# A hybrid decoder block on one core: seven products for one more unit, and two small moves from VectorE and the transfers to ScalarE and GpSimd

## The chip, the cores and the metric

The kernel runs on one core of a Trainium2 chip as one launch. The metric is the device time in microseconds (us); with one core it is that core's time. Each number is a median of runs; beside it stands one profiled execution of the same kernel, whose own time is given with its span. Engines are named as the profile does: PE is TensorE's matmul stream and PEld its weight loads, DVE is VectorE, ACT is ScalarE, POOL is GpSimd, SP is SyncE. An engine name with a q (SPq, POOLq) is the sequencer or queue that issues transfers. Five of them matter here: PE, DVE, ACT, POOL and SP's queue of loads and stores.

## The reference, cut to what matters

A sequence of 528 rows (16 meta tokens and 512 inputs, 1024 wide) is normalised and projected by one matrix `w_in` into ten parts. The first eight units of work are the eight heads of differential attention, the other eight are pairs of heads of stick-breaking attention. Both branches are gated, projected, merged and normalised.

```python
proj = jnp.einsum('bld,dn->bln', h, w_in[i])
q_d, k_d, v_d, g_d, q_s, k_s, v_s, g_s, m_d, m_s = jnp.split(proj, IN_OFFSETS, axis=-1)
...
lam = jnp.exp(jnp.sum(lp[0] * lp[1])) - jnp.exp(jnp.sum(lp[2] * lp[3])) + lam_init
...
s = jnp.einsum('bhcqd,bhckd->bhcqk', q, k).astype(jnp.float32) * (DIFF_HEAD_DIM ** -0.5)
alibi = -slopes[:, None, None] * dist.astype(jnp.float32)[None]
s = jnp.where(dist >= 0, s + alibi[None, :, None], -jnp.inf)
p = jax.nn.softmax(s, axis=-1)
a = p[:, :, 0] - lam * p[:, :, 1]
return jnp.einsum('bhqk,bhkd->bhqd', a.astype(v.dtype), v)
```

A differential head has two queries and two keys of 64 columns (c = 0 and 1), two softmax maps, and one map that is used: the first minus `lam` times the second.

## The kernel before, in words

The normalised input lies transposed in SBUF as a rounded half and a remainder (`hTh`, `hTl`), so that a product of full precision is made of three products of the rounded kind: high by high, high by low, low by high. Weights come as half tiles of 128 x 4 x 128 into tiles `raw` and are split in the same way: ACT casts the high half (L185), DVE subtracts it for the low half (L190). `prep` does this four half tiles ahead of their use and `fetch` issues the next loads on SP's queue as ring buffers come free. `names` and `items` list the half tiles in the order of use; a `rawk` tile is loaded and then has another half tile added to it, by an adding transfer on POOL's queue (L147, through `added` and `placed`).

The sixteen units follow one another. While unit u computes its scores and values, the projections of the units ahead run between its small matmuls: keys and values of unit u+1, the query of unit u+2 (`stage_q`), now and then a gate. For the units below `SEVEN`, keys and values are two plain projections (`stage_k`, `stage_v`), each of two halves of 264 columns and 24 matmuls a half (L515), 96 matmuls for a unit. From the unit `SEVEN` on, `stage_kv` makes keys and values together in seven block products of twelve matmuls (L700), 84 for a unit, in Strassen's manner: the weights' half tiles and the input's quarters are added beforehand, and the results combined by DVE (L717, L720, L722). Its input sums are made once: `input_sums(k)` for k = 0 to 3 (a POOL copy, four DVE operations of 264 columns in place in `hF`, an ACT cast into `tS`, a DVE remainder into `tl`). `SUMS_AT` says in which unit and at what point each runs, `SEVEN` also when the ring of `rawk` tiles opens (three units ahead).

`stage_q` ends with both parts of a query scaled by 0.125: ACT writes the rounded one into `A[0]`, DVE the remainder into `low` (L621, L622). The head needs them in other partitions; three transfers of 64x512 on SP's queue carry them: the second head's rounded part to `A[1][LO]`, and the two remainders to `A[1][HI]` and `A[0][HI]` (L624).

`d_scores` does the four blocks of 128 query rows, longest first (528, 400, 272, 144 keys). For each block and map: scores on PE (L764), DVE adds the bias and takes the minimum (L844), ACT takes the exponential with its row sum (L848). After both maps: the reciprocal of both sums (L852), the second map by its reciprocal and by -lambda (`nlam`, L853), and the sum of the first by its reciprocal with that (L854) into `apad`. The transposes (L776) turn `apad` for the product with the values. POOL computes the bias of the next head (L829).

Each engine's list is fixed when the program is built: a scheduler places the instructions by their dependences and its own estimate of time, `run` interleaves the steps at the points given by numbers (`TD`, `SUMS_AT`), and `keep_order` ties the instructions of PE, DVE, ACT, POOL and SP in that sequence. On the chip each engine goes through its list in order; what is not ready holds what stands behind it. The core's three banks `pj` in PSUM rotate among the projections.

Of the kernel before, what the change touches and what calls it, by code (L numbers as in the profile page):

```python
# [12 lines left out]
AF = mybir.ActivationFunctionType  # L13
ALU = mybir.AluOpType
# [14 lines left out]
AOFF = [0, 416, 832, 1248]  # L29
# [6 lines left out]

ORDERED = [mybir.EngineType.PE, mybir.EngineType.DVE, mybir.EngineType.Activation, mybir.EngineType.Pool]
WARM = 12
SEVEN = 4
SUMS_AT = {0: [8.0], 1: [5.0, 11.0], 2: [8.0]}  # L40
TD = [(0.85, 11.0, 14.5), (0.95, 13.0, 16.5)]
GATE_AT = {4: 0, 5: 1, 6: 2, 7: 3, 8: 4, 11: 5, 14: 6}
LO, HI = slice(0, 64), slice(64, 128)
# [3 lines left out]
def hybrid_block_kernel(ctx: ExitStack, tc: tile.TileContext, x, meta, emb_g, emb_b, w_in, b_gate,  # L47
                        diff_lambda, subln_g, w_br_d, w_br_s, w_out, ln_g, ln_b, out):
    nc = tc.nc
    v, s, g, pe = nc.vector, nc.scalar, nc.gpsimd, nc.tensor  # L50
# [22 lines left out]
    for u, (kind, n) in enumerate(UNITS):  # L73
        if u + 1 < len(UNITS):
            other, i = UNITS[u + 1]
# [15 lines left out]
    for n, (kind, i) in enumerate(seq):  # L91
        if kind in ("BD", "BS", "wd", "ws"):
# [6 lines left out]
            o = len(loads)  # L99
# [124 lines left out]
    def placed(work, engines=ORDERED):  # L224

        ins = nc.cur_bb.bb.instructions
        n = len(ins)
        work()
        for e in engines:
            new = next((i for i in ins[n:] if i.engine == e), None)  # L230
            old = next((ins[m] for m in range(n - 1, max(n - 400, 0), -1) if ins[m].engine == e), None)
            if new is not None and old is not None:
                follow(new, old)
# [54 lines left out]
    nlam = const.tile([P, 1], F32, name="nlam")  # L288
# [297 lines left out]
    with tc.tile_pool(name="att", bufs=1) as ap:  # L586
# [22 lines left out]
        def stage_q(unit, kind, n):  # L609

            res = []
            yield from proj_tok(res, "q" + kind, n)
            ps = res[0]
            A = [apool.tile([P, S], F32R, tag=f"A{c}", name=f"A{c}") for c in range(2)]
            if diag:
                if len(diag) == 1:
                    diag.append(ap.tile([P, L], F32R, tag="bias", name="low", bufs=2))
                low = diag[1][:, :S]
            else:
                low = gpool.tile([P, S], F32R, tag="sg", name="low")  # L620
            s.activation(A[0], ps, AF.Copy, scale=0.125)  # L621
            v.scalar_tensor_tensor(low, ps, 0.125, A[0].bitcast(F32), op0=ALU.mult, op1=ALU.subtract)  # L622
            for o, src in ((A[1][LO], A[0][HI]), (A[1][HI], low[HI]), (A[0][HI], low[LO])):
                nc.sync.dma_start(o.bitcast(F32), src.bitcast(F32))  # L624
            unit["A"] = A
            yield 0.64
# [192 lines left out]
        def d_scores(unit, h):  # L819

            A = unit["A"]


            bias = ap.tile([P, L], F32, tag="bias", name="bias", bufs=2)
            if h == 0:
                g.iota(bias, pattern=[[-1, L]], base=400, channel_multiplier=1, allow_small_or_imprecise_dtypes=True)
                g.affine_select(bias, bias, pattern=[[-1, L]], compare_op=ALU.is_ge, fill=1e30, base=400,
                                channel_multiplier=1)
            g.tensor_scalar(bias, biases[-1] if h else bias, 0.5 if h else -0.5, None, op0=ALU.mult)  # L829
            biases.append(bias)  # L830
            a = apads[h % 2]
            mn = ap.tile([P, NB, 2, 2], F32, tag="mn", name="mn", bufs=2)
            zs = ap.tile([P, NB, 2], F32, tag="zs", name="zs", bufs=2)
            rz = ap.tile([P, NB, 2], F32, tag="rz", name="rz", bufs=2)
            for i in reversed(range(NB)):
                nk = NKEY[i]
                e = [E[c][:, ZOFF[i]:ZOFF[i] + nk] for c in range(2)]
                for c in range(2):
                    m = mn[:, i, c, :]
                    for n, (ps, k0, use) in enumerate(logits(A[c], K[c], i)):  # L840
                        if n == 1:
                            yield
                        b0 = 384 - P * i + k0
                        v.tensor_tensor_reduce(e[c][:, k0:k0 + use], ps[:, :use], bias[:, b0:b0 + use], -1.0, 3e38,  # L844
                                               ALU.add, ALU.min, m[:, n:n + 1])
                    if nk > 512:
                        v.tensor_tensor(m[:, 0:1], m[:, 0:1], m[:, 1:2], op=ALU.min)
                    s.activation(e[c], e[c], AF.Exp, scale=-1.0, bias=m[:, 0:1], accum_out=zs[:, i, c:c + 1])  # L848
                    if c == 0:
                        yield  # L850
                r = rz[:, i, :]
                v.reciprocal(r, zs[:, i, :])  # L852
                v.tensor_scalar(e[1], e[1], r[:, 1:2], nlam, op0=ALU.mult, op1=ALU.mult)  # L853
                v.scalar_tensor_tensor(a[:, AOFF[i]:AOFF[i] + nk], e[0], r[:, 0:1], e[1], op0=ALU.mult, op1=ALU.add)  # L854
                yield

        def d_values(unit, ta):
# [114 lines left out]
        for u, (kind, n) in enumerate(UNITS):  # L972
# [11 lines left out]
            if u in SUMS_AT:  # L984
                if not tS:
                    tS.append(ypool.tile([P, KT, L], F32R, tag="ys", name="tS"))
                steps += [(t, lambda k=u + (u > 1) + m: placed(lambda: input_sums(k))) for m, t in enumerate(SUMS_AT[u])]
            if u in GATE_AT and u < 14:
                proj.append(raw_gate(GATE_AT[u], kept["r"][GATE_AT[u]]))
            if kind == "d":  # L990
# [167 lines left out]
    for p in range(4):  # L1158
        steps = []
# [118 lines left out]
```

## Time and profile before

| what | value |
| --- | --- |
| median of three runs | 706.77 us (705.07 to 707.03) |
| profiled execution, own time | 705.09 us |
| its span | 703.3 us |
| PE busy | 693.3 us, 99% of the span |
| DVE busy | 569.5 us, 81% |
| ACT busy | 440.5 us, 63% |
| POOL busy | 129.8 us, 18% |
| data moved by DMA | 124.93 MB, mean 178 GB/s |

Shares are of the span. "Busy" counts the time in which at least one instruction of that engine runs. Groups of instructions are read as: line, engine, operation, output <- inputs, shape, count | busy us, mean ns of one | idle time of the engine just before them and who ended it. A row of waits is: engine, tile, line <- releaser: us in all, times, longest. A row of the timeline is: start us, us, the rest. A row of busy time in a stretch has its length and then PE, PEld, DVE, ACT, POOL (each with its count), the granted clock, the DMA share and GB/s.

### The profile page before, as it was taken

The page shows a single profiled execution, that of the slowest core. Times are in us where ns is not written, and L with a number is a line of the kernel's source. Part 1 is how long each engine was busy: PE and PEld are TensorE (multiplying, and loading weights), DVE is VectorE, ACT ScalarE, POOL GpSimd, SP SyncE. Part 2 cuts the span into 40 slices and gives each one's busy share as a digit, 9 for nine tenths or more (in the row PEclk, how much of TensorE's full clock was granted, in tenths as well). Part 3 has the DMA queues.
Part 4 walks back from the last instruction along what each step waited for, and adds up shares of the span by engine and source line. Part 5 has one row for each costly group of instructions (what it writes and reads, how often), then busy time and mean ns, then how long its engine had stood idle before and what let it go on. Part 6 is the DMA issues. An engine that isn't in the chain of part 4 may idle for free.

```text
span 703.3 us, 13282 instructions
## 1 busy us (share of the span) xinstructions
PE 693.3 (99%) x4478; PEld 634.1 (90%) x4478; DVE 569.5 (81%) x1225; ACT 440.5 (63%) x1073; POOL 129.8 (18%) x140
## 2 busy tenths in 40 slices
PE   8999999999999999999999999999999999999996
PEld 8999999989899898999989899988888998999885
DVE  6887998878786777899887898977666888688887
ACT  6676767767566687777757687766555456555400
POOL 2243112222222201212121220000012201230011
PEclk9999999999999999999999999999999999999999
DMA  9399557988888796899898977547477749697702
GB/s 292 103 195 182 145 117 178 212 177 184 221 186 182 188 195 183 173 223 206 207 192 219 203 152 194 164 124 242 137 165 142 148 121 245 136 174 194 264 25 116
DMA packets 184215, 124.93 MB, mean 178 GB/s; under 512 B 8994, under 2 KB 168131, under 8 KB 184147
## 3 DMA queue, kind: packets, MB, share of 16 engines
q1 hardware_dynamic: 148050, 102.84, 50.5%
q0 software_dynamic: 35776, 20.19, 23.0%
q10 hardware_dynamic: 320, 1.06, 0.4%
q8 instruction: 35, 0.57, 0.3%
q14 instruction: 34, 0.27, 0.1%
HBM read 93.54 MB, written 9.44 MB: 146 GB/s over the span
## 4 chain that ended last, share of the span: by engine, by line
PE 93%; ACT 2%; SPq 1%; DVE 1%; DMA 1%; issue 0%; DVEq 0%; ACTq 0%
PE q L700 18%; PE ps L501 12%; PE ps L499 12%; PE ps L500 12%; PE q L1083 11%; PE pso L1206 6%; PE ps L515 6%; PE sc L764 6%; PE t L776 4%; PE tv L733 1%; PE av L931 1%; PE av L932 1%; DMA raw<-in_w_in_dram 1%; PE av L925 1%; PE av L933 1%; DMA xt<-in_x_dram 1%
## 5 line engine op out<-in xcount | busy, mean ns | idle before, releaser
L190 DVE TENSOR_TENSOR w<-raw,w 128x512 fp32r<-128x512 f32 x168 | 114.3, 689 | 37.7 <-ACT w L185 36.4
L500 PE MATMUL ps<-hTl,w 128*128 128x512 f32 x368 | 144.9, 394 | 0.0
L499 PE MATMUL ps<-hTh,w 128*128 128x512 f32 x368 | 144.7, 393 | 0.0
L501 PE MATMUL ps<-hTh,w 128*128 128x512 f32 x368 | 144.7, 393 | 0.0
L185 ACT CAST w<-raw 128x512 fp32r<-128x512 f32 x168 | 103.5, 627 | 11.6 <-PE ps L501 5.4
L147 POOL DMA_DIRECT2D rawk<-in_w_in_dram x48 | 66.1, 1630 | 119.5 <-DMA rawk<-in_w_in_dram 66.1
L700 PE MATMUL q<-tS,w 128*128 128x264 f32 x384 | 82.6, 289 | 0.0
L1083 PE MATMUL q<-gh,w 128*128 128x256 f32 x448 | 81.4, 283 | 0.2 <-ACT t L1092 0.2
L501 PEld LDWEIGHTS ps<-hTh,w 128*128 128x128 f32 x368 | 69.2, 188 | 13.5
L500 PEld LDWEIGHTS ps<-hTl,w 128*128 128x128 f32 x368 | 69.2, 188 | 13.1
L499 PEld LDWEIGHTS ps<-hTh,w 128*128 128x128 f32 x368 | 69.2, 188 | 13.0
L1083 PEld LDWEIGHTS q<-gh,w 128*128 128x128 f32 x448 | 70.2, 192 | 0.5 <-ACT t L1092 0.4
L764 PE MATMUL sc<-k,A 128*128 128x264 f32 (+3 forms) x320 | 66.0, 299 | 0.0
L700 PEld LDWEIGHTS q<-tS,w 128*128 128x128 f32 x384 | 63.7, 189 | 0.3
L1083 PE MATMUL q<-gl,w 128*128 128x256 f32 x224 | 63.5, 283 | 0.0
L700 PE MATMUL q<-hTh,w 128*128 128x264 f32 x288 | 60.8, 286 | 0.0
L916 DVE TENSOR_TENSOR_SCAN e<-e,diag 128x528 f32<-128x528 f32 (+1 forms) x64 | 54.2, 850 | 5.6 <-ACT e L910 5.6
L700 PE MATMUL q<-tl,w 128*128 128x264 f32 x192 | 54.9, 286 | 0.0
L764 PEld LDWEIGHTS sc<-k,A 128*128 128x128 f32 x320 | 50.1, 189 | 2.2
L515 PE MATMUL ps<-hTh,w 128*128 128x264 f32 x256 | 51.5, 289 | 0.2 <-ACT k L642 0.2
L700 PEld LDWEIGHTS q<-hTh,w 128*128 128x128 f32 x288 | 47.8, 189 | 1.0
L781 ACT CAST ah<-t 128x384 fp32r<-128x384 f32 (+2 forms) x72 | 34.3, 477 | 21.7 <-PE t L776 21.6
(284 smaller groups left out, 1572.1 us busy)
## 6 DMA issues: line engine op xcount, KB each, us to landing
raw<-in_w_in_dram SPq DMA_DIRECT2D x142, 256.0 KB, 3.4
rawk<-in_w_in_dram POOLq DMA_DIRECT2D x48, 256.0 KB, 5.7
rawk<-in_w_in_dram SPq DMA_DIRECT2D x36, 256.0 KB, 4.1
k<-ks SPq DMA_DIRECT2D x60, 132.0 KB, 3.0
raw<-in_w_out_dram SPq DMA_DIRECT2D x16, 256.0 KB, 4.0
k<-ks SPq DMA_DIRECT2D x60, 66.0 KB, 2.7
A<-low SPq DMA_DIRECT2D x28, 128.0 KB, 3.1
raw<-in_w_br_diff_dram SPq DMA_DIRECT2D x12, 256.0 KB, 3.3
```

The lines of the kernel that those rows point to most:

```text
L147: second[l] = [lambda raw=raw, x=x: g.dma_start(raw, x, accum_op=ALU.add) for x in more]
L185: s.copy(wh, raw)
L190: eng.tensor_tensor(wl, raw, wh.bitcast(F32), op=ALU.subtract)
L499: pe.matmul(ps, wh[:, k % 4, :], hTh[:, k, M:], start=(k == 0), stop=False)
L500: pe.matmul(ps, wh[:, k % 4, :], hTl[:, k, M:], start=False, stop=False)
L501: pe.matmul(ps, wl[:, k % 4, :], hTh[:, k, M:], start=False, stop=(k == KT - 1))
L515: pe.matmul(ps[:, :H2], a[:, k % 4, :], b[:, k, ts(c, H2)], start=(k == 0 and m == 0), stop=(k == KT - 1 and m == 2))
L700: pe.matmul(bank, a[:, k, :], b, start=start and k == 0 and j == 0, stop=k == 3 and j == 2, skip_group_check=not start)
L764: pe.matmul(ps[:, :n], q, K[:, m, k0:k0 + n], start=(m == 0), stop=(m == 1))
L916: v.tensor_tensor_scan(rev, rev, diag[0][:, L - nk:][:, ::-1], 0.0, ALU.mult, ALU.max)
L1083: pe.matmul(bank, a[:, k, :], b[:, n, k, :], start=start and k == 0 and m == 0, stop=k == 3 and m == 2, skip_group_check=not start)
L1206: pe.matmul(ps, MH[k][:, ts(t, P)] if m == "h" else ML[:, k, ts(t, P)], WO[c]["hl".index(w)][:, k, r], start=(n == 0), stop=(n == 3 * KT - 1))
```

## The change

Four edits. `SEVEN` goes from 4 to 3, so that the fourth unit (differential head 3) gets its keys and values from seven products. `SUMS_AT` now places two input sums in unit 0 and two in unit 1 (before one, two and one in units 0, 1 and 2), and the index of a sum is counted accordingly. In `stage_q` ACT writes the second head's rounded query part from PSUM into `A[1][LO]`, in place of the transfer from `A[0][HI]`. In `d_scores` POOL multiplies the second map's reciprocal by -lambda, ACT multiplies the first map by its reciprocal in place, and DVE's last operation takes the second map by that product plus the scaled first map; the separate DVE multiply of the second map is gone. Lines behind these edits move down by one or two in the changed kernel (L854 there is POOL's multiply, L855 ACT's scaling, L856 the addition).

```diff
-SEVEN = 4
-SUMS_AT = {0: [8.0], 1: [5.0, 11.0], 2: [8.0]}
+SEVEN = 3
+SUMS_AT = {0: [7.0, 12.0], 1: [4.0, 9.0]}
...
             s.activation(A[0], ps, AF.Copy, scale=0.125)
+            s.activation(A[1][LO], ps[HI], AF.Copy, scale=0.125)
             v.scalar_tensor_tensor(low, ps, 0.125, A[0].bitcast(F32), op0=ALU.mult, op1=ALU.subtract)
-            for o, src in ((A[1][LO], A[0][HI]), (A[1][HI], low[HI]), (A[0][HI], low[LO])):
+            for o, src in ((A[1][HI], low[HI]), (A[0][HI], low[LO])):
                 nc.sync.dma_start(o.bitcast(F32), src.bitcast(F32))
...
                 r = rz[:, i, :]
                 v.reciprocal(r, zs[:, i, :])
-                v.tensor_scalar(e[1], e[1], r[:, 1:2], nlam, op0=ALU.mult, op1=ALU.mult)
-                v.scalar_tensor_tensor(a[:, AOFF[i]:AOFF[i] + nk], e[0], r[:, 0:1], e[1], op0=ALU.mult, op1=ALU.add)
+                g.tensor_tensor(r[:, 1:2], r[:, 1:2], nlam, op=ALU.mult)
+                s.activation(e[0], e[0], AF.Copy, scale=r[:, 0:1])
+                v.scalar_tensor_tensor(a[:, AOFF[i]:AOFF[i] + nk], e[1], r[:, 1:2], e[0], op0=ALU.mult, op1=ALU.add)
...
-                steps += [(t, lambda k=u + (u > 1) + m: placed(lambda: input_sums(k))) for m, t in enumerate(SUMS_AT[u])]
+                steps += [(t, lambda k=2 * u + m: placed(lambda: input_sums(k))) for m, t in enumerate(SUMS_AT[u])]
```

The order on POOL, in a head of the middle of the differential part. Before, the bias of the next head and then four adding reads (`rawk`):

```order
L829 TENSOR_SCALAR bias<-bias 128x528
L147 DMA rawk<-in_w_in_dram 128x4x128 x4
L829 TENSOR_SCALAR bias<-bias 128x528
L147 DMA rawk<-in_w_in_dram 128x4x128 x3
L829 TENSOR_SCALAR bias<-bias 128x528
```

And in the changed kernel:

```order
L830 TENSOR_SCALAR bias<-bias 128x528
L854 TENSOR_TENSOR rz<-rz,nlam 128x1
L147 DMA rawk<-in_w_in_dram 128x4x128 x2
L854 TENSOR_TENSOR rz<-rz,nlam 128x1 x2
L147 DMA rawk<-in_w_in_dram 128x4x128
L854 TENSOR_TENSOR rz<-rz,nlam 128x1
L147 DMA rawk<-in_w_in_dram 128x4x128
L830 TENSOR_SCALAR bias<-bias 128x528
```

The four multiplies of a head stand among its four adding reads, and the last of them, that of the shortest block, behind the bias operation.

The order on DVE around the longest block (528 keys) of a head. `e0`, `e1` are the two maps, `rz` the reciprocals, `w2` a weight's low half. Before:

```order
L844 ISA mn_2727 128x1
L852 RECIPROCAL rz_2729<-zs_2728 128x2
L853 TENSOR_SCALAR e1_441<-e1_441,rz_2729,nlam_148 128x528
L190 TENSOR_TENSOR w2_2867<-raw_2525,w2_2867 128x512
L854 SCALAR_TENSOR_TENSOR apad0_427<-e0_440,rz_2729,e1_441 128x528
```

And in the changed kernel:

```order
L853 RECIPROCAL rz_2386<-zs_2385 128x2
L723 TENSOR_TENSOR vT_2374<-q_2372,vT_2374 128x264
L845 ISA e1_441,mn_2384<-sc_2502,bias_2382 128x400
L845 ISA mn_2384 128x1
L190 TENSOR_TENSOR w2_2554<-raw_2214,w2_2554 128x512
L856 SCALAR_TENSOR_TENSOR apad1_428<-e1_441,rz_2386,e0_440 128x528
```

The addition comes four rows behind the reciprocal; before, it was the multiply and one row.

The order on PE at the beginning of unit 2 in the changed kernel, where the second product of unit 3's keys and values ends and the next begins (`tS` and `tl` are the input sums, `t` a transpose, `sc` scores):

```order
L795 MATMUL t_1248<-ident,sx 128x128
L777 MATMUL t_1248<-ident,apad_428 128x128 x3
L765 MATMUL sc<-k_443,A_968 128x264 x4
L701 MATMUL q<-tS,w_1180 128x264
L701 MATMUL q<-tl,w_1180 128x264
L701 MATMUL q<-tS,w_1180 128x264
L765 MATMUL sc<-k_442,A_967 128x400 x2
L701 MATMUL q<-tS,w_1227 128x264
```

Where these products stand, the kernel before has matmuls of L515 on `hTh` and `hTl`, which need no input sum.

## The prediction

> **What bounds the kernel now.** I read the page first, then the waits of TensorE, then the busy time in stretches of one unit, then the chain.
>
> ```profile
> PE 693.3 (99%) x4478; PEld 634.1 (90%) x4478; DVE 569.5 (81%) x1225; ACT 440.5 (63%) x1073; POOL 129.8 (18%) x140
> ...
> PE 93%; ACT 2%; SPq 1%; DVE 1%; DMA 1%; issue 0%; DVEq 0%; ACTq 0%
> ```
>
> TensorE (PE) is busy 99% of the span and is 93% of the chain that ended last. A high share alone is not proof, so the next view is what PE waited for in the whole run:
>
> ```profile
> PE warm L309 <- POOL ident masks.py:199: 1.4, 1, 1.4
> PE bank L344 <- DVE xn L340: 1.2, 1, 1.2
> PE ps L515 <- ACT k L642: 0.2, 1, 0.2
> PE q L1083 <- ACT t L1092: 0.2, 1, 0.2
> ```
>
> The first two lie in the prologue, the others are 0.2 us each. In the eight differential heads, where all four edits lie, PE doesn't stand still. What the other engines have to spare there is seen in stretches of about one unit (PE, PEld, DVE, ACT, POOL in that order):
>
> ```profile
> 33.00:59.00 26.00, 25.95 (x191) 25.00 (x192) 21.00 (x58) 17.75 (x46) 12.70 (x13) 1.00 1.02 210
> 59.00:85.00 26.00, 26.00 (x189) 24.72 (x188) 22.04 (x64) 17.78 (x45) 5.07 (x4) 1.00 0.70 150
> 85.00:111.00 26.00, 26.00 (x190) 24.78 (x190) 22.70 (x64) 18.05 (x48) 3.80 (x3) 1.00 0.53 131
> 111.00:142.00 31.00, 31.00 (x229) 29.67 (x228) 28.60 (x84) 23.81 (x64) 8.39 (x7) 1.00 0.91 196
> 174.00:202.00 28.00, 28.00 (x184) 25.66 (x183) 21.51 (x63) 18.32 (x47) 7.08 (x5) 1.00 0.87 194
> ```
>
> PE fills every stretch; VectorE (DVE) fills 77 to 92%, ScalarE (ACT) 65 to 77%. The clock is 1.00. So a change moves the time in two ways only: by the number of matmuls, or by making something so late that PE, which goes through its list in order, has to stand.
>
> **Edit 1, matmuls.** Unit 3 gets keys and values from seven products of twelve matmuls (84) in place of 96; all have 264 columns. The chain shows what one costs when they follow each other:
>
> ```profile
> 33.05 6.06 PE ps L515 x48
> 107.28 1.46 PE q L700 x12
> 109.67 1.46 PE q L700 x12
> ```
>
> 1.46/12 is 0.122 us; 6.06/48 is 0.126 in the first stretch. Twelve fewer at 0.122 are 1.46 us; at the other end 96 x 0.126 - 84 x 0.122 = 12.10 - 10.25 = 1.85 us. The unit that changes lies near 80 to 110 us, where the quicker rate is seen, so I take 1.6 us, nearer the first. It is on the path: PE has no wait there to hand it to.
>
> **Edit 1, the other engines.** What seven products ask of DVE and ACT, and what an input sum asks:
>
> ```profile
> L190 DVE TENSOR_TENSOR w<-rawk,w 128x512 fp32r<-128x512 f32 x48 | 32.8, 684 | 6.4 <-ACT w L185 6.3
> L170 DVE TENSOR_TENSOR rawk<-rawk,raw 128x512 f32<-128x512 f32 x12 | 8.2, 683 | 0.0
> L717 DVE TENSOR_TENSOR kvt<-q,kvt 128x264 f32<-128x264 f32 x12 | 5.0, 420 | 0.1
> L677 ACT CAST tS<-hF 128x1056 fp32r<-128x1056 f32 x4 | 4.3, 1084 | 0.0
> L678 DVE TENSOR_TENSOR tl<-hF,tS 128x1056 fp32r<-128x1056 f32 x4 | 5.0, 1252 | 0.0
> ```
>
> Unit 3 has seven half tiles of weights for four: DVE gains three splits (3 x 0.684), one sum (0.683) and three combinations (3 x 0.42), 4.0 us; ACT gains three casts of much the same size and two or three copies, some 3 us. An input sum is four DVE operations of 0.42 and one of 1.25, 2.9 us, and 1.1 us of ACT. Of the four, one moves from the stretch 85:111 to 33:59. So DVE gets 2.9 us more in the first unit, nothing more in the second, and 4.0 - 2.9 = 1.1 us more in the third, before what edit 3 takes away. On the queues: two more reads of 256 KB and, on GpSimd's (POOL's), four adding reads of the same size; POOL is busy 3.80 of 26 us in that stretch and has room for 4 x 1.3 us. Cost: nothing on the path, since DVE with 28.60 of 31 us in the stretch 111:142 let PE wait for nothing; without that cover it is the second rival.
>
> **Edit 2.** Fourteen transfers of 128 KB within SBUF give way to fourteen ACT copies of 64x512 straight from PSUM.
>
> ```profile
> A<-A SPq DMA_DIRECT2D x14, 128.0 KB, 3.4
> L938 ACT COPY half<-av 64x512 f32<-64x512 f32 x16 | 9.3, 581 | 12.0 <-PE av L933 7.9 <-issue 2.6 <-ACT e L912 1.2
> ```
>
> At 0.58 us each ACT gets 8.1 us more over 14 units. The query part is there some 3.4 - 0.6 = 2.8 us sooner, but it is wanted a unit later, and PE waited for none of these transfers: worth nothing. The PSUM bank is held 0.58 us longer at most; three banks rotate. Cost 0, because ACT has 7 to 10 us free per unit.
>
> **Edit 3.** In 32 blocks DVE loses one operation, ACT gets one of the same shape, POOL gets a multiply of one column.
>
> ```profile
> L853 DVE TENSOR_SCALAR e<-e,rz,nlam x32: 342/479/718, 45.9 to 235.6; 128x528 f32<-128x528 f32 x8, 128x400 f32<-128x400 f32 x8, 128x272 f32<-128x272 f32 x8, 128x144 f32<-128x144 f32 x8
> L848 ACT ACTIVATE e<-e,mn 128x528 f32<-128x528 f32 x16 | 11.8, 740 | 3.6 <-DVE mn L847 3.6
> L893 ACT ACTIVATE r<-r 128x512 f32<-128x512 f32 x8 | 5.1, 642 | 0.1
> L299 POOL TENSOR_TENSOR lne<-xmv,epsr x3: 189/192/639, 8.7 to 15.8; 128x1 f32<-128x1 f32 x3
> L299 POOL TENSOR_TENSOR lne<-fmv,epsr x3: 190/191/1282, 681.5 to 692.3; 128x1 f32<-128x1 f32 x3
> ```
>
> DVE loses about 32 x 0.479 = 15 us, 1.9 per head. ACT's new scaling isn't in the trace; its bounds are the same engine's exponential with a pointer bias (0.740 at 528) above and a plain-scaled one (0.642 at 512) below. I take 0.74 at 528, less for shorter blocks: about 2.2 us per head, 17 us in all. ACT goes from 18.3 to about 21 of 28 us in the last stretch above, and in 85:111, with all three edits, from 18.05 to about 23 of 26 (2.2 + 0.6 + 3 more, 1.1 for the sum less): the fullest place. POOL's multiply lies between 0.19 and 1.28 us; 0.2 to 0.6 is likely. DVE's 15 us are no gain, as PE didn't wait for DVE.
>
> A rule speaks against this edit: the Trainium skill, ScalarE: Activation LUTs, "Rules for kernel authors", sends mul and add to VectorE rather than ScalarE. The rows agree at 528 columns, 0.55 us for L853 on DVE (below) against 0.74 for L848 on ACT. By the rule 0.2 us of engine time per block is lost; by the stretches above ACT has the room, and the sum stays.
>
> The new thing is the order. The addition (L854, now L856) needs a chain DVE, POOL and ACT, and DVE again, and each queue is served in order. Before, the way from one to the other and a cast of ACT looked like this:
>
> ```profile
> 193.71 0.57 DVE L844 CUSTOM_DVE_ANT_0 e<-sc,bias 128x400 f32<-128x400 f32 x1 [0.72 <-PE sc L764]
> 194.21 0.08 DVE L844 DVE_READ_ACCUMULATOR2_ANT mn<- 128x1 f32 x1
> 194.21 0.16 DVE L852 RECIPROCAL rz<-zs 128x2 f32<-128x2 f32 x1
> 194.41 0.55 DVE L853 TENSOR_SCALAR e<-e,rz,nlam 128x528 f32<-128x528 f32 x1
> 194.88 0.68 DVE L190 TENSOR_TENSOR w<-raw,w 128x512 fp32r<-128x512 f32 x1
> 195.48 0.76 DVE L854 SCALAR_TENSOR_TENSOR apad<-e,rz,e 128x528 f32<-128x528 f32 x1
> ...
> 199.74 0.41 DVE L722 TENSOR_TENSOR vT<-q,vT 128x264 f32<-128x264 f32 x1
> ```
>
> ```profile
> L185 ACT CAST w<-raw 128x512 fp32r<-128x512 f32 x168 | 103.5, 627 | 11.6 <-PE ps L501 5.4
> ```
>
> It took from 194.37 to 195.48. In the changed order four rows stand between, of the kinds L722 (0.41), L844 (0.57 and 0.08) and L190 (0.68): 1.7 us. In that time ACT can finish one cast of 0.63 and the scaling of 0.74, 1.4 us. It just fits.
>
> On POOL the multiply stands once per head behind the bias operation and elsewhere beside adding reads that may wait:
>
> ```profile
> 175.92 1.83 POOL L829 TENSOR_SCALAR bias<-bias 128x528 f32<-128x528 f32 x1 [2.43 <-DVE mn L844]
> 186.69 1.31 POOL L147 DMA_DIRECT2D rawk<-in_w_in_dram  x1 [8.94 <-DMA rawk<-in_w_in_dram]
> ```
>
> ```profile
> POOL rawk L147 <- DMA rawk<-in_w_in_dram: 66.1, 14, 8.9
> ```
>
> Behind the bias it can be 1.8 us late, once per head, on the last block. A stop of DVE up to 1 us has the free 6.5 us of a 28 us unit to vanish in, save where PE leans on DVE closely. The closest place I found:
>
> ```profile
> 199.32 0.42 DVE L720 TENSOR_TENSOR vT<-kvt,q 128x264 f32<-128x264 f32 x1
> ...
> 199.89 0.30 PE L700 MATMUL q<-hTh,w 128*128 128x264 f32 x1
> ```
>
> The seventh product accumulates into the bank that L720 reads: 199.89 - 199.74 = 0.15 us to spare. But edit 3 takes 1.9 us per head from just this queue, so it should grow.
>
> **Sum.** -1.6 (matmuls) + 0 + 0 + 0. The profiled execution took 705.1 us, span 703.3; it would be 703.5 and 701.7. The three runs' median is 706.77, 1.7 above the profiled one, so the median comes to 705.2.
>
> **Rivals.**
>
> *POOL's queue holds the reciprocal.* An adding read waits for its first half (14 times, 66.1 us, mean 4.7, longest 8.9). If a multiply comes to stand behind such a wait, DVE's addition waits, and behind it the evictions and weight splits that PE needs. At the place above 4.7 - 0.15 - 1.9 (DVE's relief in that head) = 2.7 us would reach PE; it decides from a wait of about 2 us on. In two of the eight heads that is +5.4: 705.2 + 5.4 = 710.6, slower. Against it: the order shows the reads spread between the multiplies, and their data requested long before.
>
> *The sums are just in time.* In the third unit the second product uses the fourth input sum, which now stands at the end of the unit before. Its chain is four operations of 0.42, ACT's 1.08 and DVE's 1.25, 4.0 us at best, and DVE is 85 to 87% busy in the stretches 59:111. If half of it, 2 us, is not done, PE waits once: 705.2 + 2.0 = 707.2, no change. For it: L678 is a single long row among many. Against: edit 3 frees 1.9 us in each of those units.
>
> *ACT comes late.* The scaling stands in ACT's queue behind DVE's reciprocal, so casts of weights stand behind it, and DVE already waits for those casts most:
>
> ```profile
> DVE w L190 <- ACT w L185: 55.3, 56, 4.1
> ```
>
> Mean 1.0 us. If one in four of 32 blocks gave PE 0.5 us of it: +4.0, 709.2, slower. This is what the Trainium skill's rule on ScalarE (ScalarE: Activation LUTs) would come to.
>
> *More than the matmuls.* The same 264-column matmul is seen at 0.122 and 0.126 us. If less work of DVE and fewer transfers bring the 864 matmuls of L700 down by 2 ns each, and the twelve are worth 1.85, the time is 705.2 - 1.7 - 0.25 = 703.2, faster. Against: I see no row that ties the rate to DVE.
>
> **How the numbers follow.** No change to be told from this measurement is within 0.3%, 2.1 us: 704.65 to 708.9. My forecast, 705.2 with its own range 704.3 to 706.4, has chance 0.50; the just-in-time sums 0.13; more than the matmuls 0.19; POOL's queue 0.11; late ACT 0.07. The forecast is 0.55 us from the bound, so about 0.14 of its 0.50 falls on the faster side. Faster: 0.19 + 0.14 = 0.33. Slower: 0.11 + 0.04 of late ACT = 0.15. Same: the rest, 0.52. The range 703.0 to 708.6 leaves out most of the two slow cases and the far end of the fast one.
>
> **What would show it.** Right: PE still without waits between 40 and 640 us, PE busy smaller by 1.5 to 2, L700 with 84 more matmuls and L515 with 96 fewer, DVE's busy time lower by about 11 us (15 - 4), ACT's higher by about 28. Wrong in the order: a wait of DVE at the addition on POOL's rz or ACT's e of over 1 us each, and PE rows that wait for DVE tiles kvt, vT, ah, al or tl between 78 and 240 us. A wait of PE on tl near 85 us would be the just-in-time sums; a shorter PE row for the same shape, the last rival.

## The result, and the profile after

The changed kernel takes 709.44 us (median of 6 runs, 708.91 to 709.92), the kernel before 705.50 (6 runs, 705.05 to 707.03). The ratio is 1.0050, with a 95% interval of 1.0040 to 1.0061: slower by 3.9 us, where 705.2 was forecast, 703.0 to 708.6 as the range. The profiled execution took 709.78 us with a span of 708.0; that of before had 703.3, so the two traces differ by 4.7 us.

From the page after: busy time by engine, the chain's shares, and two kinds of transfers (size in KB, median us from issue to landing).

```profile
PE 695.4 (98%) x4466; PEld 634.7 (90%) x4466; DVE 563.2 (80%) x1200; ACT 466.7 (66%) x1123; POOL 143.7 (20%) x176
...
PE 88%; DVE 4%; ACT 2%; DMA 2%; SPq 1%; issue 1%; DVEq 0%; ACTq 0%
...
k<-ks SPq DMA_DIRECT2D x60, 132.0 KB, 3.6
...
k<-ks SPq DMA_DIRECT2D x60, 66.0 KB, 3.6
```

The twelve matmuls are gone (4466 for 4478), and PE's share of the chain fell from 93% to 88%. `ks` to `k` are the key stores, a kind of transfer that the prediction didn't speak of: two parts of the next head's keys, carried within SBUF on SP's queue. A head's `k` has one buffer, so they can start only when the head before has done with its keys, and the first scores of the next head wait for them. Before, they took 3.0 and 2.7 us.

What PE waited for after, without the prologue's row and the two of 0.2 us that were there before:

```profile
PE sc L765 <- DMA k<-ks: 1.3, 1, 1.3
PE sc L765 <- ACT e L914: 1.3, 1, 1.3
PE sc L765 <- DVE mn L845: 0.6, 1, 0.6
```

Three new waits, each once, all in front of scores. Busy time in stretches of 20 us (PE, PEld, DVE, ACT, POOL), after, and one of them before:

```profile
80.00:100.00 20.00, 19.34 (x142) 18.27 (x142) 18.79 (x56) 17.27 (x42) 6.74 (x9) 1.00 0.76 164
...
120.00:140.00 20.00, 18.68 (x130) 17.43 (x129) 15.13 (x47) 16.03 (x42) 7.68 (x8) 1.00 0.85 183
...
340.00:360.00 20.00, 19.00 (x137) 18.16 (x138) 16.94 (x31) 16.75 (x46) 6.32 (x6) 1.00 0.75 175
```

```profile
340.00:360.00 20.00, 20.00 (x136) 18.60 (x135) 17.19 (x34) 15.52 (x42) 6.88 (x6) 1.00 0.87 197
```

PE lost 0.66, 1.32 and 1.00 us in these three. The clock is 1.00 in all. The third stretch has nothing of edits 1 and 3: there the stick-breaking units run.

**The largest stop** lies at 133.3 us. The chain after, in order of time (start, us, what):

```profile
130.19 0.16 SPq L654
...
130.40 4.39 DMA k<-ks
134.79 0.14 issue
134.93 0.48 PE sc L765 x2
```

PE's matmul ahead of these scores started at 133.32, and one of its shape usually lasts 0.12 us: PE stood about 1.5 us for the last key store of the head. Before, SP's row of the head's last key store and PE's row of the first scores behind the wait for it read:

```profile
129.78 0.60 SPq L653 DMA_DIRECT2D k<-ks  x1
134.61 0.41 PE L764 MATMUL sc<-k,A 128*128 128x264 f32 x2
```

By its semaphore that store landed at 132.29, 2.3 us before PE came. (The scores at 131.90 started ahead of this landing, so they don't read it.) So two things moved: PE would have come 3.0 us after the issue where it had come after 4.8, and the last store took 4.39 us (66 KB) where it had taken 2.50 (132 KB). With either of the two as before, the store would have landed before PE came. What else ran in the stretch 128 to 132 us is seen in the transfers of both kernels (queues: packets, MB, share; then the issues of that stretch). Before:

```profile
q1 hardware_dynamic: 700, 0.79, 82.6%
q0 software_dynamic: 214, 0.10, 21.3%
...
k<-ks SPq DMA_DIRECT2D x1, 66.0 KB, 2.7
```

After:

```profile
q1 hardware_dynamic: 627, 0.69, 64.4%
q0 software_dynamic: 517, 0.26, 52.0%
...
rawk<-in_w_in_dram POOLq DMA_DIRECT2D x1, 256.0 KB, 6.0
d<-yd SPq DMA_DIRECT2D x1, 256.0 KB
k<-ks SPq DMA_DIRECT2D x1, 66.0 KB, 4.4
```

POOL's adding reads (q0) moved 0.26 MB where they had moved 0.10, and SP issues a store of 256 KB (`d<-yd`) just ahead of the last two key stores, which before stood behind them. That these slowed the store is argued from the overlap; no run removed them alone. The Trainium skill (DMA: Bandwidth & Descriptors, "Issuing engines are not separate DMA queues") says that transfers of all issuing engines run on the same 16 DMA engines and interleave; the shares of q0 and q1 above, with the longer store, agree with it.

**The second stop** lies at 339.5 us, and here the row of waits names the wrong releaser. The timeline of SP and then of PE after (a row of SP spans the issuing, not the transfer):

```profile
336.19 2.13 SPq L654 DMA_DIRECT2D k<-ks  x2
```

```profile
339.34 0.41 PE L765 MATMUL sc<-k,A 128*128 128x264 f32 x2
341.00 0.48 PE L765 MATMUL sc<-k,A 128*128 128x264 f32 x2 [1.26 <-ACT e L914]
```

ACT's exponential is said to release PE. But the scores at 341.00 read the other half of the keys, and in the program they wait for the key stores. The sequencer that loads PE's weights waits from 339.44 to 340.94 for two semaphores of transfers; the later one belongs to the store issued at 336.19 (the first of the two in SP's row), which landed at 340.91. PE goes on 0.09 us later. It is the same kind of stop, 1.4 us. Before, PE came to the first scores of this unit at 337.07, 3.2 us after the last store that they wait for had landed (333.87).

**The third** lies at 88 us, where the prediction had looked. The chain after:

```profile
82.04 2.26 DMA raw<-in_w_in_dram
84.33 0.61 ACT w L185
84.97 0.69 ACT r L893
85.65 0.97 ACT tS L678
86.65 1.26 DVE tl L679
87.91 0.60 DVE w L190
88.51 0.20 DVE ax L799
88.71 0.34 DVE e L845
89.11 0.63 PE sc L765 x2
```

The last input sum is cast (`tS`) and subtracted (`tl`) at 85.65 to 87.91; PE takes `tl` at 87.96, and then waits for the minimum, which stands on DVE behind `tl` and the low half of that weight. Together PE loses 1.1 us. The head of this chain is a weight that landed late, and the input sum stands behind its cast.

1.5 + 1.4 + 1.1 are 4.0 us. From start to start of matmuls, all that exceeds the usual (the median of the same shape) by over 20 ns adds up to 19.3 us before and 25.0 after: +5.7. With the twelve matmuls gone, -1.5, that is +4.2 of the 4.7 by which the spans differ.

### The profile page after: what moved, and what is told of

Same layout as the page of the kernel before. It is cut to its first block, busy times and chain, and to the rows that moved or that the text cites. A ratio compares the mean times of both kernels' runs of the same rounds, so it can differ in the third digit from the quotient of the medians.

```text
span 708.0 us, 13314 instructions
## 1 busy us (share of the span) xinstructions
PE 695.4 (98%) x4466; PEld 634.7 (90%) x4466; DVE 563.2 (80%) x1200; ACT 466.7 (66%) x1123; POOL 143.7 (20%) x176
## 4 chain that ended last, share of the span: by engine, by line
PE 88%; DVE 4%; ACT 2%; DMA 2%; SPq 1%; issue 1%; DVEq 0%; ACTq 0%
PE q L701 18%; PE ps L500 11%; PE ps L499 11%; PE ps L501 11%; PE q L1085 11%; PE pso L1208 6%; PE sc L765 6%; PE ps L515 4%; PE t L777 3%; DVE w L190 1%; PE tv L734 1%; DMA raw<-in_w_in_dram 1%; PE av L933 1%; DMA k<-ks 1%; PE av L934 1%
## 5 line engine op out<-in xcount | busy, mean ns | idle before, releaser
L701 PE MATMUL q<-tS,w 128*128 128x264 f32 x416 | 88.0, 288 | 0.0
L147 POOL DMA_DIRECT2D rawk<-in_w_in_dram x52 | 71.4, 1625 | 32.4 <-DMA rawk<-in_w_in_dram 16.7
L701 PE MATMUL q<-hTh,w 128*128 128x264 f32 x312 | 69.0, 290 | 0.0
L701 PEld LDWEIGHTS q<-tS,w 128*128 128x128 f32 x416 | 68.5, 189 | 0.3
L918 DVE TENSOR_TENSOR_SCAN e<-e,diag 128x528 f32<-128x528 f32 (+1 forms) x64 | 53.9, 851 | 7.1 <-ACT e L912 6.9
L701 PE MATMUL q<-tl,w 128*128 128x264 f32 x208 | 59.5, 287 | 0.0
L701 PEld LDWEIGHTS q<-hTh,w 128*128 128x128 f32 x312 | 52.2, 189 | 1.1 <-ACT gr L541 0.3
L945 POOL DMA_DIRECT2D ys<-half x14 | 11.7, 839 | 193.1 <-ACT sx L771 85.8
L701 PE MATMUL q<-hTl,w 128*128 128x264 f32 x156 | 45.1, 289 | 0.0
```

What stands on the lines that cost most here:

```text
L147: second[l] = [lambda raw=raw, x=x: g.dma_start(raw, x, accum_op=ALU.add) for x in more]
L701: pe.matmul(bank, a[:, k, :], b, start=start and k == 0 and j == 0, stop=k == 3 and j == 2, skip_group_check=not start)
L918: v.tensor_tensor_scan(rev, rev, diag[0][:, L - nk:][:, ::-1], 0.0, ALU.mult, ALU.max)
```

## The experiments

Three theories stood after this. A: edit 1 crowds the beginning of unit 2 (input sums, late weight). B: the moves to ACT and POOL (edits 2 and 3) cost PE time through their queues. C: each edit, however small, makes the scheduler write all five lists anew, and in the new lists PE comes to some scores before the key stores that they wait for have landed; the work itself costs next to nothing.

### One edit at a time

`seven` is edit 1 alone, `query` edit 2, `maps` edit 3, `query_maps` 2 and 3.

In `seven`, with the index of the sums:

```diff
-SEVEN = 4
-SUMS_AT = {0: [8.0], 1: [5.0, 11.0], 2: [8.0]}
+SEVEN = 3
+SUMS_AT = {0: [7.0, 12.0], 1: [4.0, 9.0]}
```

In `query`:

```diff
+            s.activation(A[1][LO], ps[HI], AF.Copy, scale=0.125)
-            for o, src in ((A[1][LO], A[0][HI]), (A[1][HI], low[HI]), (A[0][HI], low[LO])):
+            for o, src in ((A[1][HI], low[HI]), (A[0][HI], low[LO])):
```

In `maps`, with the operands of the addition changed to match:

```diff
-                v.tensor_scalar(e[1], e[1], r[:, 1:2], nlam, op0=ALU.mult, op1=ALU.mult)
+                g.tensor_tensor(r[:, 1:2], r[:, 1:2], nlam, op=ALU.mult)
+                s.activation(e[0], e[0], AF.Copy, scale=r[:, 0:1])
```

> Edit 1 alone (seven products for unit 3, sums in units 0 and 1). Theory A, the waits come from edit 1's crowding of units 1 to 3: the stops of PE near 88 us (1.1 us, sums and a late weight load) and near 133 us (1.5 us, key stores) are there without edits 2 and 3, the one near 339 us is not; -1.5 for the matmuls and +3.1 for the stops in 80 to 140 us make about +1.6 us against the kernel before. Theory B, the waits come from edits 2 and 3, which load ACT's list and put POOL and ACT between reciprocal and addition: no stop over 0.5 us, -1.5 us. Theory C, every edit has the scheduler write new lists and each list has its own few stops: between -1.5 and +3, with stops at places of its own.

> Edit 2 alone (ACT writes the second head's query part). A: no change, within 0.5 us, PE without stops. B: ACT's copy stands ahead of casts and scores' sigmoids, so the stop of 1.4 us near 339 us is there, +1 to +1.5 us. C: stops at places of its own, 0 to +2 us.

> Edit 3 alone (POOL scales the reciprocal, ACT the first map). A: no change, within 0.5 us. B: DVE's additions wait and PE stops in the eight heads, +2 to +4 us. C: stops at places of its own, 0 to +2 us.

> Edits 2 and 3 together, without edit 1. A: within 0.5 us, since the stops near 88 and 133 us belong to edit 1. B: the changed kernel's time plus the twelve matmuls, +5 us. C: not the sum of the two alone; stops where neither alone has them.

Against 705.55 (21 runs of the kernel before, 704.84 to 706.58):

| kernel | median us | ratio (95%) | largest stop of PE in the trace (us, at) |
| --- | --- | --- | --- |
| seven | 707.71 | 1.0035 (1.0023 to 1.0046) | 1.3 at 59.6, key store |
| query | 706.35 | 1.0013 (1.0005 to 1.0022) | 1.0 at 402.6, key store |
| maps | 708.13 | 1.0040 (1.0026 to 1.0053) | 2.5 at 338.5, key store |
| query_maps | 708.12 | 1.0033 (1.0020 to 1.0046) | 1.1 at 338.3, key store |

Every edit alone is slower, and the medians alone add up to +5.5 us, more than the change as a whole. Theory A falls: `seven` has no stop near 88 or 133 us, and `maps`, without edit 1, loses 2.6 us. PE's largest waits in `seven` and in `maps`:

```profile
PE sc L764 <- DMA k<-ks: 1.2, 1, 1.2
```

```profile
PE sc L764 <- DMA k<-ks: 2.3, 1, 2.3
```

The largest stop of each kernel is for a key store, in `seven`, `query` and `maps` each at another place. (In `query` the row of waits names ACT's exponential; the last store landed at 403.45, and PE went on at 403.59.) In `maps` it lies past 330 us, where no differential head runs any more (the maps of edit 3 end at 236 us). The chain of `maps` there:

```profile
329.70 7.47 DMA k<-ks
...
337.63 3.29 DMA k<-ks
```

A store of the same size that takes 3 us in most places took 7.5. The profiled run of `maps` was its slowest (711.87; its runs go from 706.88 on), so the size of that stop is not the median's. Read as lists (operation, tiles and shape of each row), `maps` and `query` differ from before in dozens of places of PE's list, `maps` in about twice as many as `query`, though PE's instructions are the same ones in both: they were only put in another order. This speaks for C, but a cost of the moved work (B) isn't separated yet.

### The same edits with the lists held

In these kernels each engine's list is written down and tied together after the program is built. The list is that of the kernel before; ACT's new instruction stands right behind the one that it follows in the code, the dropped one leaves no gap, and POOL's multiply keeps DVE's old place in time. PE's list is unchanged, row by row.

```diff
+    def held_lists():
+        ...
+        for k in order_of_before:
+            for ins in slots[k]:
+                follow(ins, before[ins.engine])
+                before[ins.engine] = ins
```

`after_held` takes the list of `seven` instead and puts edits 2 and 3 into it. In kernels with held lists lines lie 25 to 28 further on: L790 and L792 are the scores of L764, L725 and L726 the products of L700.

> Edit 2 alone, with the five engines' lists held to those of the kernel before: ACT's copy stands right behind the first one, the transfer is left out, nothing else moves. Theory C (the time is lost by new lists): no change, within 0.5 us, no stop of PE over 0.5 us between 40 and 640 us. Theory B (the moved work itself costs): +0.8 us as with edit 2 alone, the stop near 402 us is there.

> Edit 3 alone, with the lists held: POOL's multiply and ACT's scaling stand at the time at which DVE's multiply stood, the addition keeps its place. C: within 0.7 us of the kernel before, no stop of PE over 0.5 us, although DVE waits for ACT at many of the 32 additions. B: +2.6 us as with edit 3 alone.

> Edits 2 and 3 together, with the lists held. C: within 0.7 us of the kernel before. B: +2.6 us as without held lists.

> All four edits; the lists are those of edit 1 alone, with edits 2 and 3 put in at their places. C: the time of edit 1 alone, 707.7 us, within 0.7 us, with its stops near 59 and 108 to 125 us and without those near 88, 133 and 339 us. B: the changed kernel's 709.4 us.

Against 705.69 (27 runs, 704.80 to 707.06):

| kernel | median us | ratio (95%) | with free lists |
| --- | --- | --- | --- |
| query_held | 706.34 | 1.0012 (1.0003 to 1.0021) | 1.0013 |
| maps_held | 706.24 | 1.0008 (0.9999 to 1.0018) | 1.0040 |
| query_maps_held | 706.79 | 1.0021 (1.0012 to 1.0030) | 1.0033 |
| after_held | 707.82 | 1.0033 (1.0020 to 1.0045) | 1.0050 |

All of PE's waits in `query_maps_held`:

```profile
PE warm L334 <- POOL ident masks.py:199: 1.4, 1, 1.4
PE bank L369 <- DVE xn L365: 0.7, 1, 0.7
PE ps L540 <- ACT k L670: 0.2, 1, 0.2
PE q L1114 <- ACT t L1123: 0.2, 1, 0.2
```

These are the four rows of the kernel before: no key store, no exponential, no minimum. From 33 us on, PE's instructions run with a shift against the kernel before that changes by more than 0.1 us at one place only, by 0.34 us at 171.1 us. There the seventh product waits for DVE's combination (L720 before), one unit ahead of the place of 0.15 us that the prediction had named as the closest. The combination is late because the addition in front of it waits for ACT's scaling:

```profile
170.52 0.63 DVE L885 SCALAR_TENSOR_TENSOR apad<-e,rz,e 128x400 f32<-128x400 f32 x1 [0.90 <-ACT e L883]
```

The 132 KB key stores take 3.0 us in it and in `query_held`, 2.8 in `maps_held`, as before; in all lists that were written anew, 3.3 to 3.7.

So most of what `maps` lost is the list: 1.0040 free and 1.0008 held, with intervals apart. For the two edits together the intervals overlap. For edit 2 alone it is the same both ways: its +0.65 us is not the list's, and as its profiled run keeps step with that of before from 41 to 490 us, it isn't seen where this arises. What is left to B is the 1.1 us of `query_maps_held` (0.8 to 2.1 by the interval). That, and the 0.65 of `query_held`, are more than C allowed (0.7 and 0.5): the moved work isn't free. One stop of 0.8 us in `maps_held`, in the last unit, was also in `maps` and not in `query_maps_held`; its cause stays open.

`after_held` comes out at the time of edit 1 alone, as C has it, and lacks the stops near 88, 133 and 339 us. It keeps three stops of edit 1's list, near 108, 123 and 125 us (the one of `seven` near 59 us isn't in its trace); two are named:

```profile
PE ms L916 <- ACT sx L798: 1.0, 1, 1.0
PE sc L792 <- DVE mn L872: 0.5, 1, 0.5
```

### The lists mended, the work as in the change

If C holds, the changed kernel must come back to about the time of before when only places in its lists change. `after_mended` has the lists of the changed kernel with these moves: the scores that stood at 133 us twelve matmuls later, those at 341 us nine matmuls and four transposes later, ACT's cast of the last input sum ahead of the late weight's, and on DVE its remainder, `ax` and the minimum ahead of that weight's low half. On ACT and DVE these moves read:

```
 ACTIVATE A<-ps 64x512
+CAST tS<-hF 128x2x528
 CAST w<-raw 128x512
 ACTIVATE r<-ms,epsr 128x512
-CAST tS<-hF 128x2x528
```

```
-TENSOR_TENSOR w<-raw,w 128x512
...
 TENSOR_TENSOR tl<-hF,tS 128x1056
-TENSOR_TENSOR w<-rawk,w 128x512
 TENSOR_TENSOR ax<-t,own_block 128x128
 ISA e,mn<-sc,bias 128x264
 ISA mn 128x1
+TENSOR_TENSOR w<-raw,w 128x512
+TENSOR_TENSOR w<-rawk,w 128x512
```

`seven_mended` does the same for the stops of `seven`: the first scores of unit 1 five matmuls and four transposes later, the third load of that place behind two key stores, and one product `ms` (L885) moved to the next one. `same_work` asks the opposite: nothing of the change, but a number that sets the order.

```diff
same_work:
-TD = [(0.85, 11.0, 14.5), (0.95, 13.0, 16.5)]
+TD = [(0.85, 11.0, 15.2), (0.95, 13.0, 16.5)]
```

> All four edits, the changed kernel's own lists with three places mended: PE's first scores on keys that come by transfer stand twelve matmuls (near 133 us) and nine matmuls and four transposes (near 341 us) later, and near 88 us ACT casts the last input sum before the late weight, DVE takes its remainder before that weight's low half. Work and instructions are the same. Theory C, the loss is the stops, and the stops are places in the lists: the stops of 1.1, 1.5 and 1.4 us go, 709.4 - 4.0 = 705.4 us, within 0.8. If the stops are not the loss, or each only moves to the next wait: above 708 us.

> Edit 1 alone with two places of its own lists mended: near 60 us the first scores of unit 1 stand five matmuls and four transposes later and two key stores before a weight load, near 108 us the sum of squares stands twelve matmuls later. C: 707.7 - 1.3 - 0.5 = 705.9 us, within 0.7; what is left of the stops lies near 124 us (0.9 us). Otherwise above 707 us.

> The kernel before with one number of its order changed (the product with the values of a head is put in 0.7 units of the order's time later, in the heads without a gate), so that the scheduler writes other lists for the same instructions. C: the time moves though no work does, somewhere from -0.3 to +2.5 us, and what it loses is in stops of PE, most likely at scores that wait for key stores. If lists don't matter: within 0.5 us and no stop over 0.5 us.

Against 705.59 (24 runs, 705.09 to 707.17): `after_mended` 706.26, 1.0008 (0.9999 to 1.0016); `seven_mended` 707.70, 1.0029 (1.0016 to 1.0042); `same_work` 706.89, 1.0017 (1.0009 to 1.0026).

`after_mended` gives back 3.2 us without a change of work; 4.0 were expected. One wait is left between the prologue and the last units:

```profile
PE q L726 <- ACT kvt L737: 0.6, 1, 0.6
```

`same_work` is 1.3 us slower than before with the very same instructions, put in another order in dozens of places of PE's list. `seven_mended` is a miss: its stops are gone from the trace but for the same wait for `kvt`, and the profiled run took 706.90, yet its median is that of `seven` (707.71). In both of these the profiled run is near the low end of the runs (705.89 of 705.81 to 708.63, and 706.90 of 706.74 to 709.82), and the trace shows no stop of the missing size. Where the other runs lose their time isn't seen in any trace here. So for edit 1 by itself C is not shown.

### The last places

`after_mended2` moves the copy of the first product (`kvt`, L712 in the changed kernel) on ACT directly behind the cast `tS`, a gate copy ahead of another copy, and the scores near 339 us three matmuls later.

```
 L703 CAST tS<-hF 128x2x528
+L737 COPY kvt<-q 128x264
 L186 CAST w_1371<-raw 128x512
 L918 ACTIVATE r<-ms,epsr 128x512
```

> The lists of after_mended with the next waits mended too: ACT copies the first product of unit 3 out of its bank right behind the last input sum (0.75 us near 88 us), and a gate's copy stands ahead of a wait for VectorE (0.25 us near 255 us); near 339 us the scores on the first half of the keys stand three matmuls later as well (0.15 us). Theory C: PE without a stop over 0.3 us between 40 and 640 us, the twelve matmuls show, 706.3 - 1.1 = 705.2 us, within 0.7; against the kernel before -0.4 us. If waits go on from place to place: no better than 706.3 us.

It was a miss: 709.14 us against 705.83 (11 runs), 1.0043 (1.0029 to 1.0057). PE's largest wait and the copy on ACT's timeline:

```profile
PE t L820 <- ACT r L918: 2.3, 1, 2.3
```

```profile
87.36 0.38 ACT L737 COPY kvt<-q 128x264 f32<-128x264 f32 x1 [2.26 <-DVE tl L704]
```

The tile `kvt` takes over the buffer of the last input sum, so the copy can't start before DVE has made the remainder `tl`. ACT stood 2.26 us at its head, and the norm L918 behind it, which had nothing to do with it, held PE's transposes for 2.3 us. With the two other moves the median is 2.9 us above that of `after_mended`, and the only stop of this size in the trace is that of one copy of 0.38 us at the wrong place in a list.

`after_mended3` puts this copy behind the norm's second operation (L920):

```
-L737 COPY kvt<-q 128x264
 L186 CAST w_1371<-raw 128x512
 L918 ACTIVATE r<-ms,epsr 128x512
 L186 CAST w_1408<-rawk 128x512
 L920 ACTIVATE r<-r 128x512
+L737 COPY kvt<-q 128x264
```

With it went `before_held`, the kernel before with its own lists written down, to see what holding a list costs by itself.

> As after_mended2, with ACT's copy of the first product out of its bank (L712) between the two operations of the norm instead of ahead of them. In after_mended2 PE stood 2.3 us near 86 us for the norm behind that copy, and the copy waited 2.3 us for the remainder of the last input sum: its tile is the buffer in which that sum was formed. If this dependence is what is left, the stop near 86 us goes, no stop over 0.3 us stays between 40 and 640 us, and the time is 706.3 - 1.1 = 705.2 us, within 0.7. If the start of unit 2 is too full for any order, a stop of 0.5 to 1.5 us stays near 86 to 92 us: 705.8 us or more.

> The kernel before with its own lists written down, as the kernels with held lists have them: the same instructions in the same lists. Both theories: no change, within 0.4 us. If it comes out 0.5 us or more above the kernel before, so much of the held kernels' +0.6 to +1.1 us belongs to the way of holding and not to edits 2 and 3.

Against 705.68 (21 runs): `after_mended3` 705.97, 1.0007 (0.9996 to 1.0018); `before_held` 705.55, 1.0003 (0.9994 to 1.0012). Holding costs nothing that can be told from these runs. `after_mended3` is 0.8 us above its expected 705.2. One wait is left in its heads, of the first scores of unit 3 for the remainder of their query (`A<-low`). Its two transfers were issued from 105.38 on by SP, and the second landed at 109.99:

```profile
105.38 1.18 SPq L650 DMA_DIRECT2D A<-low  x2
```

```profile
110.08 0.72 PE L790 MATMUL sc<-k,A 128*128 128x264 f32 x4 [0.87 <-issue]
```

`after_mended4` lets these four matmuls come three matmuls and seven transposes later:

```
-MATMUL sc<-k,A 128x264 x4
 MATMUL q<-tS,w 128x264
...
 MATMUL t<-ident,apad 128x128 x3
 MATMUL t<-ident,apad 128x128 x3
+MATMUL sc<-k,A 128x264 x4
```

> As after_mended3, with the first scores of unit 3 three matmuls and seven transposes later on PE, since they stood 1.0 us near 109 us for the transfers of the query's remainder. Theory C: the last stop goes, 706.0 - 0.9 = 705.1 us, within 0.7; against the kernel before -0.5 us, the first sight of the twelve matmuls. If the saved matmuls only bring PE sooner to what it waits for: again 705.7 us or more, with a stop of about 1 us at a place of its own.

It took 705.12 us (11 runs, 704.76 to 706.05) against 705.69 (15 runs): 0.9995 (0.9986 to 1.0004). All of PE's waits, and the three stretches shown above:

```profile
PE warm L334 <- POOL ident masks.py:199: 1.4, 1, 1.4
PE ps L540 <- ACT k L668: 0.2, 1, 0.2
PE q L1110 <- ACT t L1119: 0.2, 1, 0.2
```

```profile
80.00:100.00 20.00, 20.00 (x146) 19.04 (x145) 18.66 (x53) 17.25 (x43) 6.29 (x9) 1.00 0.70 156
...
120.00:140.00 20.00, 20.00 (x142) 18.89 (x141) 16.71 (x53) 17.32 (x47) 7.87 (x9) 1.00 0.90 191
...
340.00:360.00 20.00, 20.00 (x144) 18.89 (x143) 19.52 (x36) 17.31 (x47) 7.02 (x6) 1.00 0.89 193
```

PE is full again. The kernel does exactly the work of the changed one, and is 4.3 us faster than it by moves in the lists alone. Its 132 KB key stores still take 3.7 us: what the moves changed is when PE asks for them. Whether it beats the kernel before can't be told: the interval holds 1. The 1.5 us of twelve matmuls would be 0.998 and lie outside it, so part of them is still lost, and it isn't shown where. The 1.1 us that edits 2 and 3 cost with held lists (`query_maps_held`) are of the missing size; that they are the same loss is not shown.

## Why the prediction was wrong

**The step that failed** is the sum "-1.6 (matmuls) + 0 + 0 + 0". Its zeros were worked out with all other instructions where they stood before. They didn't stand there: the scheduler wrote all lists anew (PE's differs in dozens of places), and by that the change got 4.0 us of stops in front of scores. `after_mended4` shows that the same work in mended lists is 4.3 us faster, and the pair `maps` and `maps_held` that one edit loses most of its time by its list and not by its work. The zero for the work of edits 2 and 3 was off as well, by about 1.1 us (`query_maps_held`).

That `after_mended4` takes 705.12, the forecast's number, is luck. The forecast was 1.6 us less than 706.77, a median of three runs; in all later sets the kernel before took 705.5 to 705.8. Against that `after_mended4` saves 0.6 us, with an interval that reaches down to nothing. In the same way the miss is 5.5 us of change (-1.6 forecast, +3.9 measured), not the 4.2 between 705.2 and 709.44.

**What it did not look at.** It named the place with the least to spare as "199.89 - 199.74 = 0.15 us to spare". One of this kind, a unit earlier, did give way in `query_maps_held`, for 0.34 us. But it listed only DVE's side. The key stores, with one buffer for `k`, were a second set of places where PE meets another engine's work: two of the three stops after are there, and so is the largest one of each edit alone. The time to spare in the trace of before would not have named these two: by its landing times they had 2.3 and 3.2 us, while the scores at 307.5 us had 0.8 and did not become a stop. The order of the changed kernel was read at three places only, none of them a head's first scores.

**Edit 1, matmuls.** Right in count: L515 has 96 fewer, L700 (now L701) 84 more. That they are "on the path" holds only where PE is full; "PE busy smaller by 1.5 to 2" was wrong, PE's busy time rose from 693.3 to 695.4. It can't show so little: kernels with the very matmuls of before have 693.3 (before) to 697.6 (`maps`).

**Edit 1, the other engines.** "Cost: nothing on the path, since DVE with 28.60 of 31 us in the stretch 111:142 let PE wait for nothing" was wrong by the third stop, 1.1 us, and by the list. A share of a stretch does not say whether the one operation that PE needs next stands behind another. DVE's own time fell by 6.3 us and not by 11. Both terms were off: in `seven` alone it rises by 6.7 us (576.2 for 569.5) where 4.0 were counted, and in `maps` alone it falls by 10.4 (559.1) where 15 were. ACT rose by 26.2, forecast 28.

**Edit 2.** "Worth nothing" is near: 706.35 free and 706.34 held, 0.7 to 0.8 us slower than before in both, with intervals that leave out zero by little. ACT's copy took 0.595 us, forecast 0.58.

**Edit 3.** What ACT and POOL get was forecast well: ACT's scaling takes 0.41 to 0.75 us (0.74 taken for 528 columns), POOL's multiply 0.18 to 0.56 (0.2 to 0.6). The order that "just fits" did fit. The addition L856 waited 0.6 us for POOL and 0.2 for ACT in the whole run, and POOL itself waits for the reciprocal, not the other way:

```profile
L856 DVE SCALAR_TENSOR_TENSOR apad<-e,rz,e 128x528 f32<-128x528 f32 (+3 forms) x32 | 18.0, 563 | 1.0 <-POOL rz L854 0.6 <-ACT e L855 0.2
```

With the list held the edit costs 0.55 us, with an interval that reaches down to none (0.9999). The rule of the Trainium skill (ScalarE: Activation LUTs, "Rules for kernel authors") by which a multiply belongs on VectorE would have kept this edit out; in time of the engines the trace agrees with it, in the kernel's time it is worth no more than that.

**The rivals.** *POOL's queue* falls: 0.6 us of waiting in one place. With held lists DVE waits 3.5 us for POOL in four places (`query_maps_held`), and PE for none of them. *ACT late* is seen once, by way of DVE: the 0.34 us at 171 us in `query_maps_held`, not the 4.0 that it was given. *More than the matmuls* falls. Its sum was also wrong: L700 has 12 x 84 = 1008 matmuls before and 1092 after, not 864, so with 2 ns each its time would have been some 702.8, outside the range. *The sums just in time* had the right place: the stop near 88 us is 1.1 of the 4.0 us, forecast as 2.0, at the cast and remainder that it named. PE's wait on `tl`, its sign, is only 0.2 of it; the rest is for the minimum behind `tl`. It is behind a late weight, which it didn't name. What made up most of the loss, that all lists change, was not among the rivals.

## What to carry to other kernels

Where a scheduler writes the lists, the price of an edit is the price of its work plus that of a new list, and here the second was the larger: up to +2.6 us for an edit whose work costs about 0.5. Before forecasting "no change", list every place where an engine at 99% meets a single-buffered tile or a transfer, and read the new order at each of them: compare the time to spare with the spread of that transfer (here 2.4 to 6.7 us for one size), for places with 2 and 3 us to spare gave way. To learn what the edit itself is worth, hold the old lists and add only the new instructions; to learn what it could be worth, move the consumers in the new lists to where their data are.

## What the runs showed of the hardware

- A transfer within SBUF of 66 or 132 KB takes 2.7 to 3.0 us in the median of the kernel before. Single ones of 132 KB take 2.4 to 6.7 us there, and up to 8.1 us in `maps`. With the lists of before the 132 KB median stays at 2.8 to 3.0; in the new lists it is 3.3 to 3.7, for the same transfers.
- The profile may name the wrong releaser where an instruction waits for several things: at 341.00 us it says ACT, while the last key store had landed at 340.91.
- Two kernels with the same instructions in another order differ by 1.3 us in the median (`same_work`, 1.0017, 1.0009 to 1.0026), without a stop in the trace that was taken.
